# Latent attention pipelined by a group: scores ahead of the older group's values, full-height score products, VectorE normalises

## The chip, the cores and the metric

One of the cores of a Trainium2 chip runs the whole program. The time is the device time of one execution in microseconds (us); lower is better. A core has TensorE (PE; its weight loads are shown apart as PEld), VectorE (DVE), ScalarE (ACT), GpSimd (POOL), SyncE (SP, which here only issues transfers) and 16 DMA engines. TensorE's clock is granted at one of two levels, 1.2 and 2.4 GHz; a mean of 0.5 in a stretch is the lower one throughout.

## The reference, cut to what matters

One layer of a diffusion backbone over 256 context tokens and 1024 latent tokens of width 1024: a windowed grouped-query attention (8 query heads of 64, 2 key groups) and a gated linear recurrence side by side, an output projection, then an expert retrieval that reads, for each token, 128 rows of one table and 128 rows of another. The change touches the attention. For the latent tokens it is

```python
q, k = apply_rope(q), apply_rope(k)
# blocks of 128 queries against the block, its two neighbours (|q - k| <= 128) and 256 cached context keys
s_band = einsum('bnqkgd,bnckd->bkgnqc', qb, k_band) * 64 ** -0.5      # masked outside the window
s_ctx  = einsum('bnqkgd,bckd->bkgnqc', qb, k_ctx) * 64 ** -0.5
p = softmax(concat([s_band, s_ctx, sink]))                            # the sink is a learned logit per head
o = einsum('bkgnqc,bnckd->bnqkgd', p_band, v_band) + einsum('bkgnqc,bckd->bnqkgd', p_ctx, v_ctx)
```

and for the context tokens it is the same over all 256 context tokens, without rotary, window or cache.

## The kernel before

The program is one straight list of instructions, written in this order: the modulation vectors, the context tokens from projection to retrieval (their attention from 125.6 us in the profile), the latent tokens' projection and recurrence (until 518 us), their attention (536.4 to 788.5 us), the output projection `finish` (to about 970 us), the choice of experts, and a long dense stage that computes six of the eight latent tiles' experts with all experts' weights (from about 1790 us to the end). A planner turns the list into one queue for each engine: it takes instructions in the order of the program where their inputs and buffers are ready by its own cost estimates, and so lets later ones go ahead where an engine would idle. On the chip every engine then works its queue in order.

`attend` (lines 385 to 462) does both attentions; `lat` tells them apart. It goes over tiles `t` of 128 queries and over the two key groups `g`. The four heads `c` of a group share its keys. A score product of the latent attention is split for precision: `kh` and `kl` are the high and the low part of the keys (lines 392 to 401), `qs` holds the high part of the queries in the 64 rows of its group and the low part in the other 64 rows (lines 410, 411). A head's scores (128 queries by 640 keys, 512 for the first and the last tile) lie in two PSUM banks. Each bank gets a product of 128 rows, `qs` with `kh`, which holds the keys twice (line 429), and one of 64 rows, high part of `qs` with `kl` (line 430). Two small products add the window's mask (line 433). Then VectorE takes the maximum (436) and makes the bias (437), ScalarE takes the exponential with its sum (438). After four heads the denominator follows (440 to 443), and each head is multiplied by its reciprocal (444 to 448): by `NORM = "AAGV"` the first two on ScalarE, the third on GpSimd, the fourth on VectorE. In the context attention ScalarE does all four.

The second half of a group goes over its blocks of 128 keys (lines 450 to 460): four transposes of probabilities into one PSUM tile `pt`, a copy by ScalarE to `pT`, and a product with the values into `po`. That is called a value step here. The copy of `po` into `qT` (461) ends the group. PSUM is full: three score tiles of two banks, one `pt`, one `po`.

Beside this runs a background stream, `mix` (lines 819 to 851): for four tiles of tokens 256 gather steps each. A step is an indirect transfer of 128 rows of 4 KB, issued by GpSimd (lines 830 and 841), and one VectorE instruction on what has landed (lines 833 and 847). `tick(us)` (lines 110 to 124) decides where in the program these steps stand: it adds to a clock and lets one step go for each 1.9 on it (4.0 in the choice of experts, none while `spread` runs, 2.0 in the dense stage, where the clock starts from 0; lines 53 to 55). The attention ticks 13 after each group (462), `finish` 14 after each tile (525), the choice of experts 13.6 for each of 16 blocks (571). In the dense stage a step's VectorE instruction stands behind the instruction that ticked. What is left in the queue at the end is let go at once (line 1009).

Of the kernel before, what the change touches and what calls it, by code (L numbers as in the profile page):

```python
# [9 lines left out]
F32 = mybir.dt.float32  # L10
# [5 lines left out]
AF = mybir.ActivationFunctionType  # L16
OP = mybir.AluOpType
AX = mybir.AxisListType
# [3 lines left out]
P = 128  # L22
# [14 lines left out]
SCALE = HD ** -0.5  # L37
# [19 lines left out]
E_US = 3.0  # L57
PE_US = 15.8

NORM = "AAGV"  # L60
G_SCALE = 32768.0


# [1 line left out]
def body(ctx: ExitStack, tc: tile.TileContext, i, o):  # L65
    nc = tc.nc
    V, A, T, G = nc.vector, nc.scalar, nc.tensor, nc.gpsimd
# [42 lines left out]
    def tick(us, ins=None):  # L110

        clock[0] += us
        if ins is not None:
            behind.append(ins.ins)
        ph = cur[0]
        step = D_STEP if ph == "dense" else STEP.get(ph, F_STEP)
        while queue and clock[0] >= step:
            try:
                next(queue[0])
                clock[0] -= step  # L120
            except StopIteration:
                queue.pop(0)
        if not queue:
            clock[0] = 0.0
# [213 lines left out]
    def recur(cond, st, ps, gy, xr, blocks=range(4)):  # L338
        lat, _, S, _, _, _, NB = dims(cond)
        for c in blocks:  # L340
# [42 lines left out]
            V.tensor_tensor(hs[0], hs[0], hs[1], op=OP.add)  # L383
            V.tensor_tensor(gy[:, c, :], hs[0], gy[:, c, :], op=OP.mult)
    def attend(cond, st, ps, tiles, qT, kT, vv, spare=None):
        lat, _, S, n, _, _, _ = dims(cond)
        base = S_CTX if lat else 0
        if lat:
            vc = load("vc", [P, 2, P], st)

            flat = [x.rearrange("p k t -> p (k t)") for x in spare]
            kh = flat[0][:, 0:2 * (S + base)].rearrange("p (g k) -> p g k", g=2)
            kl = flat[1][:, 0:S + base]
            qsp = [flat[1][:, S + base + n * 1024:S + base + (n + 1) * 1024].rearrange("p (g c q) -> p g c q", g=2, c=4)
                   for n in range(2)]
            half = [slice(0, 64), slice(64, 128)]
            for src, ks in ((kc, slice(0, base)), (kT, slice(base, base + S))):
                for g in range(2):
                    for r in range(2):
                        A.activation(kh[half[r], g, ks], src[half[g]], AF.Copy)  # L400
                    V.tensor_tensor(kl[half[g], ks], src[half[g]], kh[half[g], g, ks], op=OP.subtract)
        for t in tiles:
            ts = slice(t * P, (t + 1) * P)
            lo, hi = (max(t - 1, 0), min(t + 1, n - 1)) if lat else (0, n - 1)
            W = (hi - lo + 1) * P + base
            nk = W // P
            if lat:
                qs = qsp[t % 2]
                for g in range(2):
                    A.activation(qs[half[g], g], qT[half[g], :, ts], AF.Copy)  # L410
                    V.tensor_tensor(qs[half[1 - g], g], qT[half[g], :, ts], qs[half[g], g], op=OP.subtract)
            for g in range(2):
                gs = slice(g * 64, g * 64 + 64)
                pr = st.tile([P, 4, W], F32, name="pr", bufs=2)
                negm = st.tile([P, 4], F32, name="negm", bufs=2)
                sums = st.tile([P, 4], F32, name="sums", bufs=2)
                den = st.tile([P, 4], F32, name="den", bufs=2)
                for c in range(4):
                    h = g * 4 + c
                    s = ps.tile([P, 2, 512] if lat else [P, W], F32, name="s", bufs=3 if lat else 2)  # L420
                    qh = qT[gs, c, ts]

                    if not lat:
                        T.matmul(s, qh, kT[gs, 0:W], start=True, stop=True)
                    if lat:
                        k0 = base + lo * P
                        for bank, c0, k, w in ((0, 512 - base, 0, base), (1, 0, k0, W - base)):
                            out = s[:, bank, c0:c0 + w]
                            T.matmul(out, qs[:, g, c], kh[:, g, k:k + w], start=True, stop=False, skip_group_check=True)
                            T.matmul(out, qs[gs, g, c], kl[gs, k:k + w], start=False, stop=(bank == 0), skip_group_check=True)  # L430
                        edges = [(blk - lo, mi) for blk, mi in ((t - 1, 0), (t + 1, 1)) if lo <= blk <= hi]
                        for x, (blk, mi) in enumerate(edges):
                            T.matmul(s[:, 1, blk * P:(blk + 1) * P], identb, maskb[:, mi], start=False,
                                     stop=(x == len(edges) - 1), skip_group_check=True)
                        s = s.rearrange("p b w -> p (b w)")[:, 512 - base:512 - base + W]
                    V.reduce_max(den[:, c:c + 1], s, axis=AX.X)
                    V.tensor_scalar(negm[:, c:c + 1], den[:, c:c + 1], -SCALE, nsink[:, h:h + 1], op0=OP.mult, op1=OP.min)
                    A.activation(pr[:, c], s, AF.Exp,
                                 bias=negm[:, c:c + 1], scale=SCALE, accum_out=sums[:, c:c + 1])
                V.tensor_tensor(den, sink[:, g * 4:g * 4 + 4], negm, op=OP.add)  # L440
                A.activation(den, den, AF.Exp)
                V.tensor_tensor(den, den, sums, op=OP.add)
                V.reciprocal(den, den)
                for c in range(4):
                    if not lat or NORM[c] == "A":
                        A.activation(pr[:, c], pr[:, c], AF.Copy, scale=den[:, c:c + 1])
                    else:
                        {"V": V, "G": G}[NORM[c]].tensor_scalar(pr[:, c], pr[:, c], den[:, c:c + 1], None, op0=OP.mult)
                po = ps.tile([P, 4, P], F32, name="po")
                for j in range(nk):  # L450
                    pt = ps.tile([P, 4, P], F32, name="pt")
                    for c in range(4):
                        T.transpose(pt[:, c], pr[:, c, j * P:(j + 1) * P], ident)
                    pT = st.tile([P, 4, P], F32, name="pT", bufs=3)
                    A.activation(pT, pt, AF.Copy)
                    if lat and j < 2:
                        vb = vc[:, j, gs]
                    else:
                        vb = vv[:, lo + j - (2 if lat else 0), gs]
                    T.matmul(po[gs], vb, pT, start=(j == 0), stop=(j == nk - 1))  # L460
                A.activation(qT[gs, :, ts], po[gs], AF.Copy)
                tick(13)

    def finish(es, cond, tiles, qT, gy, dest):

# [224 lines left out]
    ahead = [n * (EARLY // GROUP) % len(order) < EARLY // GROUP for n in range(len(order))]  # L690
# [165 lines left out]
    with ExitStack() as ms:  # L856
# [12 lines left out]
        with ExitStack() as fs:  # L869
# [3 lines left out]
            with ExitStack() as e2:  # L873
                fo = pool(e2, "cfo")
                qT = fo.tile([P, 4, S_CTX], F32, name="qT")
                gy = fo.tile([P, 4, S_CTX], F32, name="gy")
                with ExitStack() as es:
                    fi = pool(es, "cfi")
                    kT = fi.tile([P, S_CTX], F32, name="kT")
                    vv = fi.tile([P, N_CTX, P], F32, name="vv")  # L880
# [16 lines left out]
                    st = pool(es, "cat")  # L897
                    ps = pool(es, "cps", space=PSUM)
# [18 lines left out]
    with ExitStack() as fs:  # L917
        fo = pool(fs, "lfo")
        qT = fo.tile([P, 4, S_LAT], F32, name="qT")
        gy = fo.tile([P, 4, S_LAT], F32, name="gy")  # L920
        with ExitStack() as ks:
            kv = pool(ks, "lkv")
            kT = kv.tile([P, S_LAT], F32, name="kT")
            vv = kv.tile([P, N_LAT, P], F32, name="vv")
# [40 lines left out]
            with ExitStack() as es:  # L965
                attend(1, pool(es, "lat"), pool(es, "lps", space=PSUM), range(N_LAT), qT, kT, vv, (hha, hla))
# [130 lines left out]
```

## Time and profile before

| | us |
|---|---|
| median of 3 runs (lowest, highest) | 3695.29 (3680.69, 3700.97) |
| profiled execution, its own time | 3691.55 |
| span of that execution in the profile | 3689.7 |
| TensorE busy, of the span | 3323.2 (90%) |
| VectorE busy | 3082.3 (84%) |
| GpSimd busy | 1728.7 (47%) |
| ScalarE busy | 1456.6 (39%) |

The span runs from the first to the last instruction. A busy share over the whole program is an average over stages that are limited by different things, so the stages are read one by one. Products on TensorE overlap and their ends are modelled: the distance of two starts tells more than a duration. In a timeline a line is start, duration, engine, line of the kernel, operation, output<-inputs, shape and count, and in brackets how long the engine was idle before it and what ended that.

### The profile page before, as it was taken

The page shows a single profiled execution, that of the slowest core. Times are in us where ns is not written, and L with a number is a line of the kernel's source. Part 1 is how long each engine was busy: PE and PEld are TensorE (multiplying, and loading weights), DVE is VectorE, ACT ScalarE, POOL GpSimd, SP SyncE. Part 2 cuts the span into 40 slices and gives each one's busy share as a digit, 9 for nine tenths or more (in the row PEclk, how much of TensorE's full clock was granted, in tenths as well). Part 3 has the DMA queues.
Part 4 walks back from the last instruction along what each step waited for, and adds up shares of the span by engine and source line. Part 5 has one row for each costly group of instructions (what it writes and reads, how often), then busy time and mean ns, then how long its engine had stood idle before and what let it go on. Part 6 is the DMA issues. An engine that isn't in the chain of part 4 may idle for free.

```text
span 3689.7 us, 48648 instructions
## 1 busy us (share of the span) xinstructions
PE 3323.2 (90%) x16982; PEld 2733.0 (74%) x16982; DVE 3082.3 (84%) x6710; ACT 1456.6 (39%) x2270; POOL 1728.7 (47%) x1162
## 2 busy tenths in 40 slices
PE   7888879888798988889899999989989999999995
PEld 4477654433598877779788888878878888887884
DVE  4549986767799999970699999989989998988898
ACT  5744645533211344542333333433333333333333
POOL 0012454556621121212366666656657666665663
PEclk8799989999899999999999999999999999999998
DMA  8342653568830256773799999988889998988885
GB/s 333 109 158 84 211 201 127 159 233 283 287 97 28 66 152 203 215 218 125 278 346 331 339 341 337 337 307 317 319 300 343 349 344 303 343 303 308 302 317 200
DMA packets 349142, 918.20 MB, mean 249 GB/s; under 512 B 29144, under 2 KB 150104, under 8 KB 345824
## 3 DMA queue, kind: packets, MB, share of 16 engines
q0 software_dynamic: 147456, 536.94, 41.3%
q1 hardware_dynamic: 201440, 378.16, 30.1%
q8 instruction: 133, 2.18, 0.2%
q14 instruction: 113, 0.93, 0.1%
HBM read 834.48 MB, written 80.50 MB: 248 GB/s over the span
## 4 chain that ended last, share of the span: by engine, by line
PE 33%; DVE 24%; issue 6%; DMA 3%; POOL 2%; ACT 1%; POOLq 0%; DVEq 0%; SPq 0%; ACTq 0%
PE u L140 6%; PE u L139 6%; PE u L138 6%; DVE row L833 4%; DVE acc L847 4%; PE rot L138 3%; PE rot L140 3%; PE rot L139 3%; DVE acc L742 2%; DVE oh L676 2%; PE res L138 2%; PE res L140 2%; PE res L139 2%; DVE oh L674 1%; DVE oh L677 1%
## 5 line engine op out<-in xcount | busy, mean ns | idle before, releaser
L830 POOL DMA_INDIRECT row<-in_peer_u,eid x512 | 732.6, 1431 | 571.1 <-DVE row L833 219.0
L841 POOL DMA_INDIRECT row<-in_peer_v,eid x512 | 716.3, 1399 | 493.1 <-DVE acc L847 226.9
L140 PE MATMUL u<-hh,ul 128*128 128x384 f32 x2048 | 709.2, 347 | 59.0 <-DVE ul L135 55.7
L138 PE MATMUL u<-hh,uh 128*128 128x384 f32 x2048 | 709.9, 347 | 6.2 <-ACT a L997 4.4
L139 PE MATMUL u<-hl,uh 128*128 128x384 f32 x2048 | 708.1, 346 | 0.0
L847 DVE SCALAR_TENSOR_TENSOR acc<-row,w,acc 128x1024 f32<-128x1024 f32 x508 | 655.9, 1291 | 25.8 <-DMA row<-in_peer_v,eid 24.3
L833 DVE SCALAR_TENSOR_TENSOR row<-row,h 128x1024 f32<-128x1024 f32 x512 | 623.9, 1233 | 56.6 <-DMA row<-in_peer_u,eid 56.4
L741 ACT ACTIVATE q<-rot 128x512 f32<-128x512 f32 x504 | 298.5, 596 | 479.7 <-PE rot L140 258.6
L140 PEld LDWEIGHTS u<-hh,ul 128*128 128x128 f32 x2048 | 396.7, 194 | 67.7 <-DVE ul L135 59.5
L138 PE MATMUL rot<-vh,ah 128*128 128x512 f32 x1024 | 408.5, 399 | 15.3 <-ACT q L741 14.9
L138 PEld LDWEIGHTS u<-hh,uh 128*128 128x128 f32 x2048 | 397.0, 194 | 14.2 <-ACT a L997 5.7
L139 PE MATMUL rot<-vl,ah 128*128 128x512 f32 x1024 | 400.9, 391 | 0.0
L139 PEld LDWEIGHTS u<-hl,uh 128*128 128x128 f32 x2048 | 396.7, 194 | 5.6
L140 PE MATMUL rot<-vh,al 128*128 128x512 f32 x1024 | 400.8, 392 | 0.0
L742 DVE TENSOR_TENSOR acc<-q,acc 128x512 f32<-128x512 f32 x504 | 342.7, 688 | 13.9 <-ACT q L741 12.4
L135 POOL TENSOR_TENSOR ul<-u,uh 128x1024 fp32r<-128x1024 f32 x44 | 120.6, 2741 | 427.1 <-ACT uh L134 404.2
L138 PE MATMUL mm<-hh,wh 128*128 128x256 f32 (+2 forms) x848 | 288.0, 340 | 12.9 <-ACT wh L134 12.9
L140 PE MATMUL mm<-hh,wl 128*128 128x256 f32 (+2 forms) x848 | 290.3, 343 | 7.4 <-POOL wl L135 4.7
L139 PE MATMUL mm<-hl,wh 128*128 128x256 f32 (+2 forms) x848 | 285.6, 337 | 0.0
L135 DVE TENSOR_TENSOR vl<-v,vh 128x1024 fp32r<-128x1024 f32 x128 | 156.3, 1221 | 120.4 <-DMA gt<-gd 115.9
L134 ACT ACTIVATE uh<-u 128x1024 fp32r<-128x1024 f32 x128 | 135.7, 1061 | 294.2 <-PE u L139 235.5
L138 PEld LDWEIGHTS rot<-vh,ah 128*128 128x128 f32 x1024 | 193.3, 189 | 74.3 <-ACT q L741 36.3
(260 smaller groups left out, 6079.1 us busy)
## 6 DMA issues: line engine op xcount, KB each, us to landing
u<-in_ut SPq DMA_DIRECT2D x128, 512.0 KB
v<-in_peer_v SPq DMA_DIRECT2D x128, 512.0 KB
gd<-stg SPq DMA_DIRECT2D x12, 4096.0 KB
gt<-gd SPq DMA_DIRECT2D x64, 768.0 KB
w<-in_w_mod SPq DMA_DIRECT2D x24, 1024.0 KB
ad<-a SPq DMA_DIRECT2D x88, 192.0 KB
a<-ad SPq DMA_DIRECT2D x44, 384.0 KB
w<-in_w_query SPq DMA_DIRECT2D x32, 512.0 KB
```

Of the source, the lines that this page charges most:

```text
L134: A.activation(hi, src, AF.Copy)
L135: return (eng or V).tensor_tensor(lo, src, hi, op=OP.subtract)
L138: T.matmul(out, lhs[0], rhs[0], start=first, stop=False)
L139: T.matmul(out, lhs[0], rhs[1], start=False, stop=False)
L140: T.matmul(out, lhs[1], rhs[0], start=False, stop=last)
L676: V.tensor_tensor(oh.rearrange(four, j=2), o2.rearrange(four, j=2), pairs(gh, ts), op=OP.mult)
L741: A.activation(q, p, AF.Copy)
L742: tick(share / (2 * (N_DENSE - N_RES)), V.tensor_tensor(y, q, y, op=OP.add))
L830: G.indirect_dma_start(out=u, out_offset=None, in_=i["peer_u"], in_offset=bass.IndirectOffsetOnAxis(ap=eid[:, k:k + 1], axis=0))
L833: V.scalar_tensor_tensor(u, u, 1.0, h2, op0=OP.mult, op1=OP.mult, accum_out=act[:, j:j + 1])
L841: G.indirect_dma_start(out=v, out_offset=None, in_=i["peer_v"], in_offset=bass.IndirectOffsetOnAxis(ap=eid[:, k:k + 1], axis=0))
L847: V.scalar_tensor_tensor(acc, v, w[:, j:j + 1], acc, op0=OP.mult, op1=OP.add)
```

## The change

`attend` is rewritten, in five respects.

1. Its two halves become functions, `scores(t, g)` and `values(t, g, ...)`. The loop calls `scores` for a group and then `values` for the group before it. `pr` (the probabilities of a group) gets three buffers in the latent attention, `pT` two.
2. `kl` becomes as tall as `kh`: the low part of a group's keys is copied to the other 64 rows too, by ScalarE. The second product of a bank takes all 128 rows of `qs`, so it multiplies the low part of the queries with `kl` as well. `qs` of the even tiles moves to the other spare buffer.
3. `NORM` is `"VVVV"`: VectorE normalises all four heads in the latent attention. The context attention keeps ScalarE.
4. One `po` tile serves both groups of a tile of queries, each in its own 64 rows.
5. `tick(13)` after a group becomes `tick(1.6)` after each head and `tick(1.3)` after each value step.

The order of the program changes in the context attention as well.

```diff
-NORM = "AAGV"
+NORM = "VVVV"
...
-            kh = flat[0][:, 0:2 * (S + base)].rearrange("p (g k) -> p g k", g=2)
-            kl = flat[1][:, 0:S + base]
...
+            K2 = 2 * (S + base)
+            kh, kl = (x[:, 0:K2].rearrange("p (g k) -> p g k", g=2) for x in flat)
+            qsp = [x[:, K2:K2 + 1024].rearrange("p (g c q) -> p g c q", g=2, c=4) for x in flat]
...
-                    V.tensor_tensor(kl[half[g], ks], src[half[g]], kh[half[g], g, ks], op=OP.subtract)
+                    V.tensor_tensor(kl[half[g], g, ks], src[half[g]], kh[half[g], g, ks], op=OP.subtract)
+                    A.activation(kl[half[1 - g], g, ks], kl[half[g], g, ks].bitcast(F32), AF.Copy)
...
+        def scores(t, g):
...
+            pr = st.tile([P, 4, W], F32, name="pr", bufs=3 if lat else 2)
...
-                            T.matmul(out, qs[gs, g, c], kl[gs, k:k + w], start=False, stop=(bank == 0), skip_group_check=True)
+                        T.matmul(out, qh, kl[:, g, k:k + w], start=False, stop=(bank == 0), skip_group_check=True)
...
+                tick(1.6)
...
-                        {"V": V, "G": G}[NORM[c]].tensor_scalar(pr[:, c], pr[:, c], den[:, c:c + 1], None, op0=OP.mult)
+                    V.tensor_scalar(pr[:, c], pr[:, c], den[:, c:c + 1], None, op0=OP.mult)
...
+        def values(t, g, pr, lo, nk):
...
+            if g == 0:
+                outs[t] = ps.tile([P, 4, P], F32, name="po")
+            po = outs[t]
...
+                pT = st.tile([P, 4, P], F32, name="pT", bufs=2 if lat else 3)
...
+                tick(1.3)
...
-                tick(13)
...
+        ahead = None
+        for t, g in ((t, g) for t in tiles for g in range(2)):
+            now = scores(t, g)
+            if ahead:
+                values(*ahead)
+            ahead = now
+        values(*ahead)
```

## Rows read from the trace of the kernel before

**Rows 1.** Timeline at the start of the latent attention.
```profile
530.10 4.27 ACT L400 ACTIVATE hh<-kT 64x1024 fp32r<-64x1024 f32 x4
...
536.40 0.58 PE L429 MATMUL s<-hh,hl 128*128 128x256 f32 x1 [16.03 <-DVE hl L411]
```
**Rows 2.** Busy us (instructions) by stage: PE, PEld, DVE, ACT, POOL; clock, DMA share, GB/s.
```profile
125.60:182.70 57.10, 47.49 (x118) 21.50 (x117) 32.76 (x105) 36.63 (x90) 2.20 (x4) 0.61 0.16 51
...
556.70:788.50 231.80, 205.34 (x781) 95.70 (x781) 157.34 (x286) 131.12 (x266) 115.62 (x84) 0.96 0.48 153
...
789.00:1000.00 211.00, 163.42 (x504) 91.98 (x502) 155.21 (x264) 61.16 (x116) 136.34 (x105) 0.90 0.86 293
1000.00:1600.00 600.00, 546.81 (x3986) 502.14 (x3985) 584.67 (x2692) 222.97 (x301) 127.58 (x54) 0.96 0.45 134
3643.00:3690.00 47.00, 14.53 (x54) 10.96 (x54) 38.90 (x59) 15.74 (x28) 15.91 (x9) 0.70 0.23 90
```
**Rows 3.** Timeline, weight loads of one head's scores and of the next one's first.
```profile
646.52 0.19 PEld L429 LDWEIGHTS s<-hh,hl 128*128 128x128 f32 x1
...
647.52 0.18 PEld L430 LDWEIGHTS s<-hl 64*128 64x128 f32 x1 [0.18 <-issue]
...
647.96 0.19 PEld L429 LDWEIGHTS s<-hh,hl 128*128 128x128 f32 x1
```
**Rows 4.** Timeline, weight loads among full-height products: of 256 columns, then of 384.
```profile
1131.07 0.19 PEld L139 LDWEIGHTS mm<-hl,wh 128*128 128x128 f32 x1
...
1131.19 0.19 PEld L140 LDWEIGHTS mm<-hh,wl 128*128 128x128 f32 x1
...
1999.87 0.19 PEld L139 LDWEIGHTS u<-hl,uh 128*128 128x128 f32 x1
...
2000.04 0.19 PEld L140 LDWEIGHTS u<-hh,ul 128*128 128x128 f32 x1
```
**Rows 5.** Timeline, a value step near the end of the latent attention, no scores left.
```profile
782.68 1.07 PE L460 MATMUL po<-pT,vc 128*64 128x512 f32 x2 [0.75 <-ACT pT L455]
...
783.68 0.42 PEld L453 LDWEIGHTS pt<-ident,pr 128*128 128x128 f32 x4 [0.81 <-issue]
...
784.43 0.60 ACT L455 ACTIVATE pT<-pt 128x512 f32<-128x512 f32 x1 [1.81 <-PE pt L453]
...
785.08 1.07 PE L460 MATMUL po<-pT,vv 128*64 128x512 f32 x2 [0.75 <-ACT pT L455]
```
**Rows 6.** By operation, 534 to 790 us: busy, mean ns | idle before, what ended it.
```profile
L448 POOL TENSOR_SCALAR pr<-pr,den 128x640 f32<-128x640 f32 x12 | 28.1, 2341 | 22.2 <-DVE den L443 13.8 <-DVE negm L437 8.2
...
L448 DVE TENSOR_SCALAR pr<-pr,den 128x640 f32<-128x640 f32 x12 | 9.6, 796 | 0.0
```
**Rows 7.** Timeline, one normalise on VectorE that begins before GpSimd's.
```profile
637.48 0.55 DVE L448 TENSOR_SCALAR pr<-pr,den 128x640 f32<-128x640 f32 x1
```
**Rows 8.** Timeline, SyncE issues the loads of the context tokens' output weights.
```profile
182.70 4.11 SPq L476 DMA_DIRECT2D w<-in_w_out  x8
```
**Rows 9.** Timeline, the last gather product on VectorE.
```profile
3646.40 1.28 DVE L847 SCALAR_TENSOR_TENSOR acc<-row,w,acc 128x1024 f32<-128x1024 f32 x1
```
**Rows 10.** Waits, 789 to 935 us: total us, times, longest.
```profile
DVE acc L847 <- DMA row<-in_peer_v,eid: 18.1, 15, 4.1
...
DVE row L833 <- DMA row<-in_peer_u,eid: 16.1, 13, 2.9
```
**Rows 11.** VectorE in the attention: L833 (product and its accumulator read), then L847.
```profile
536.40:788.50 252.10, 38.93 (x64) 0.93 0.47 151
...
536.40:788.50 252.10, 51.47 (x40) 0.93 0.47 151
```
**Rows 12.** Timeline of the context attention, at the lower clock: value products, then transposes.
```profile
151.37 1.97 PE L460 MATMUL po<-pT,vv 128*64 128x512 f32 x2
153.27 1.12 PE L453 MATMUL pt<-ident,pr 128*128 128x128 f32 x4
```
**Rows 13.** Busy us by stage, as in rows 2, of 15 us in the latent attention.
```profile
737.00:752.00 15.00, 15.00 (x42) 6.85 (x43) 6.95 (x17) 5.32 (x12) 5.71 (x4) 0.66 0.44 140
```

More of the change, by code (lines that the diff above doesn't have):

```diff
@@ L387, in attend @@
         base = S_CTX if lat else 0
+        half = [slice(0, 64), slice(64, 128)]
         if lat:
@@ L391, in attend @@
             flat = [x.rearrange("p k t -> p (k t)") for x in spare]
-            kh = flat[0][:, 0:2 * (S + base)].rearrange("p (g k) -> p g k", g=2)
-            kl = flat[1][:, 0:S + base]
-            qsp = [flat[1][:, S + base + n * 1024:S + base + (n + 1) * 1024].rearrange("p (g c q) -> p g c q", g=2, c=4)
-                   for n in range(2)]
-            half = [slice(0, 64), slice(64, 128)]
+            K2 = 2 * (S + base)
+            kh, kl = (x[:, 0:K2].rearrange("p (g k) -> p g k", g=2) for x in flat)
+            qsp = [x[:, K2:K2 + 1024].rearrange("p (g c q) -> p g c q", g=2, c=4) for x in flat]
             for src, ks in ((kc, slice(0, base)), (kT, slice(base, base + S))):
@@ L400, in attend @@
                         A.activation(kh[half[r], g, ks], src[half[g]], AF.Copy)
-                    V.tensor_tensor(kl[half[g], ks], src[half[g]], kh[half[g], g, ks], op=OP.subtract)
-        for t in tiles:
+                    V.tensor_tensor(kl[half[g], g, ks], src[half[g]], kh[half[g], g, ks], op=OP.subtract)
+                    A.activation(kl[half[1 - g], g, ks], kl[half[g], g, ks].bitcast(F32), AF.Copy)
+        def scores(t, g):
             ts = slice(t * P, (t + 1) * P)
@@ L405, in attend @@
             W = (hi - lo + 1) * P + base
-            nk = W // P
-            if lat:
+            gs = half[g]
+            if lat and g == 0:
                 qs = qsp[t % 2]
[L409 to L417, printed above, removed]
-                for c in range(4):
[L419 to L429, printed above, removed]
-                            T.matmul(out, qs[gs, g, c], kl[gs, k:k + w], start=False, stop=(bank == 0), skip_group_check=True)
[L431 to L447, printed above, removed]
-                        {"V": V, "G": G}[NORM[c]].tensor_scalar(pr[:, c], pr[:, c], den[:, c:c + 1], None, op0=OP.mult)
[L449 to L461, printed above, removed]
-                tick(13)
@@ new lines, in scores @@
+                for g2 in range(2):
+                    A.activation(qs[half[g2], g2], qT[half[g2], :, ts], AF.Copy)
+                    V.tensor_tensor(qs[half[1 - g2], g2], qT[half[g2], :, ts], qs[half[g2], g2], op=OP.subtract)
+            pr = st.tile([P, 4, W], F32, name="pr", bufs=3 if lat else 2)
+            negm = st.tile([P, 4], F32, name="negm", bufs=2)
+            sums = st.tile([P, 4], F32, name="sums", bufs=2)
+            den = st.tile([P, 4], F32, name="den", bufs=2)
+            for c in range(4):
+                h = g * 4 + c
+                s = ps.tile([P, 2, 512] if lat else [P, W], F32, name="s", bufs=3 if lat else 2)
+                if not lat:
+                    T.matmul(s, qT[gs, c, ts], kT[gs, 0:W], start=True, stop=True)
+                if lat:
+                    qh = qsp[t % 2][:, g, c]
+                    k0 = base + lo * P
+                    edges = [(blk - lo, mi) for blk, mi in ((t - 1, 0), (t + 1, 1)) if lo <= blk <= hi]
+                    for bank, c0, k, w in ((0, 512 - base, 0, base), (1, 0, k0, W - base)):
+                        out = s[:, bank, c0:c0 + w]
+                        T.matmul(out, qh, kh[:, g, k:k + w], start=True, stop=False, skip_group_check=True)
+                        T.matmul(out, qh, kl[:, g, k:k + w], start=False, stop=(bank == 0), skip_group_check=True)
+                    for x, (blk, mi) in enumerate(edges):
+                        T.matmul(s[:, 1, blk * P:(blk + 1) * P], identb, maskb[:, mi], start=False,
+                                 stop=(x == len(edges) - 1), skip_group_check=True)
+                    s = s.rearrange("p b w -> p (b w)")[:, 512 - base:512 - base + W]
+                V.reduce_max(den[:, c:c + 1], s, axis=AX.X)
+                V.tensor_scalar(negm[:, c:c + 1], den[:, c:c + 1], -SCALE, nsink[:, h:h + 1], op0=OP.mult, op1=OP.min)
+                A.activation(pr[:, c], s, AF.Exp,
+                             bias=negm[:, c:c + 1], scale=SCALE, accum_out=sums[:, c:c + 1])
+                tick(1.6)
@@ new lines, in scores @@
+            V.tensor_tensor(den, sink[:, g * 4:g * 4 + 4], negm, op=OP.add)
+            A.activation(den, den, AF.Exp)
+            V.tensor_tensor(den, den, sums, op=OP.add)
+            V.reciprocal(den, den)
+            for c in range(4):
+                if not lat or NORM[c] == "A":
+                    A.activation(pr[:, c], pr[:, c], AF.Copy, scale=den[:, c:c + 1])
+                else:
+                    V.tensor_scalar(pr[:, c], pr[:, c], den[:, c:c + 1], None, op0=OP.mult)
+            return t, g, pr, lo, W // P
@@ new lines, in attend @@
+        outs = {}
+        def values(t, g, pr, lo, nk):
+            ts = slice(t * P, (t + 1) * P)
+            gs = half[g]
+            if g == 0:
+                outs[t] = ps.tile([P, 4, P], F32, name="po")
+            po = outs[t]
+            for j in range(nk):
+                vb = vc[:, j, gs] if lat and j < 2 else vv[:, lo + j - (2 if lat else 0), gs]
+                pt = ps.tile([P, 4, P], F32, name="pt")
+                for c in range(4):
+                    T.transpose(pt[:, c], pr[:, c, j * P:(j + 1) * P], ident)
+                pT = st.tile([P, 4, P], F32, name="pT", bufs=2 if lat else 3)
+                A.activation(pT, pt, AF.Copy)
+                T.matmul(po[gs], vb, pT, start=(j == 0), stop=(j == nk - 1))
+                tick(1.3)
+            A.activation(qT[gs, :, ts], po[gs], AF.Copy)
```

## The prediction

> **What bounds the kernel now.** I read the page first, then the busy time by stage, then the timeline of the stage that the change rewrites, then the lists by operation and by wait. The latent attention begins with a score product at 536.40 us [rows 1] and ends at 788.5 us. In its main part, 231.8 us, TensorE is busy for 205.3 us, VectorE for 157.3 and ScalarE for 131.1 [rows 2]: TensorE bounds it. The reader should see three things in its timeline.
>
> First, the products of one head take 1.44 us from weight load to weight load, and the half-height load among them starts 0.18 us late with nothing for it to wait for but TensorE's own running product [rows 3]: products of full and of half height do not overlap. Elsewhere, where all are of full height, a 256-column product follows the last after 0.12 us and a 384-column one after 0.17, although each brings a weight load of 0.19 us [rows 4]. Secondly, where no scores are left to fill the gaps, a value step (four transposes, ScalarE's copy, the pair of value products) takes 785.08 - 782.68 = 2.40 us, with the copy of 0.60 us between transposes and product [rows 5]. Thirdly, the stage has 76 such steps (6 query tiles x 2 groups x 5 key blocks, and 2 x 2 x 4 at the edges): a step takes 231.8 / 76 = 3.05 us now. In the timeline the score products already stand between the value steps of the older group, though the program writes them later: the planner overlaps them today as well.
>
> What a step needs of TensorE now: 1.00 us for the products (782.68 to 783.68) and 0.42 for the loads of the transposes [rows 5], plus 64 heads / 76 x 1.44 = 1.21. That is 2.63; it takes 3.05, so 0.42 us stay unfilled.
>
> **The change part by part.** *Full-height products.* A head becomes 2 x 0.12 + 2 x 0.17 = 0.58 us by [rows 4], and its two mask products, which I take at up to 0.22: 0.80 us. A step then needs 1.42 + 0.84 x 0.80 = 2.09 us of TensorE. That is under the 2.40 of the bare chain, which becomes the floor. With the unfilled 0.42 added to the need it would be 2.51. There are no fewer products; low part of q times low part of k is added, at no column.
>
> *The copies for it.* kl gets a second half: four more ScalarE copies ahead of the first product, two of 256 columns and two of 1024. One of 1024 costs 4.27 / 4 = 1.07 us [rows 1]; one of 256 I estimate at 0.43: 3.0 us. TensorE already waits 16.03 us there [rows 1], so they lie on the path. Against that the first four heads are shorter, each by about 1 us at the low clock of that stretch. The 20.3 us from 536.4 to the first transposes at 556.7 change by between -7 and +3; I take -2.
>
> *VectorE normalises all four heads.* ScalarE loses two passes of each group, GpSimd one of up to 2.34 us, for whose input it idles while gathers queue behind it [rows 6]. Neither engine sets the end, so nothing is gained there directly. VectorE gets 48 passes more: 36 of 640 elements at 0.55 us, as one takes when GpSimd isn't at its own pass [rows 7], and 12 of 512 at some 0.48: 25.6 us. Its 12 present passes of 640 average 0.80 us [rows 6] as GpSimd works beside them; without that they save about 3. Net +22 us, 0.29 per step. VectorE's need per step rises from 157.3 / 76 = 2.07 to 2.36. Queued behind four normalises (2.2 us) on VectorE are the next group's maxima, which free the score buffers, and the gather products; three score buffers and a group of lead cover that. But at 2.5 us a step VectorE is 94% busy where it was 68%. I take a step at 2.55: the 2.51 and a little for this. Main part: 76 x 2.55 = 194, so **-38 us**; the ends are 2.40, which gives -49, and 2.86 (below), which gives -14.
>
> *Order and buffers.* Scores of the next group now have the earlier place in the program; the third pr buffer holds what is ahead. The value output is one bank for both groups of a tile, so the next tile's first product waits for ScalarE's copy out of it, as each group's does now. pT with two buffers suffices, since the one pt buffer lets only one step be under way. These I cost at nothing, the score products hide them; without that cover the copy of about 0.6 us would show once per tile, 5 us in all.
>
> *The context attention* (125.6 to 182.7 us) gets the new order too, not the other edits. It runs at a mean clock of 0.61 with TensorE busy for 47.5 of 57.1 us [rows 2], beside the preparation of the latent tokens. Its end matters: the loads of w_out are issued at 182.70 [rows 8]. The idle 9.6 us bound the gain, near enough; I take -4 (-12 to +3).
>
> *Gathers one by one.* The ticks of the stage fall from 16 x 13 = 208 to 64 x 1.6 + 76 x 1.3 = 201.2. At 1.9 a step, with the 112 of the next stage, and then 217.6 at 4.0, 222 gather steps are let go before the dense stage now and 218 then. The four go to the end of the dense stage, whose ticks (1629 at 2.0) have 814 places for 802 steps now, 806 then. VectorE works for 38.9 of the last 47 us [rows 2], and the last gather product stands at 3646.40 [rows 9], just ahead of the closing sums: four more at 1.28 us land among these. **+5 us** (0 to +6). Before that, a shorter attention leaves the background gathers less room. What doesn't fit falls into stages where the DMA engines are 86% busy (789 to 1000 us) or VectorE 97% (1000 to 1600) [rows 2]: +4 (0 to +20).
>
> **Sum**: -38 - 2 - 4 + 5 + 4 = -35 us. The profiled execution took 3691.55 us, 3.7 below the median of 3695.29; so 3656.5 for it and **3660 us** for the median.
>
> **The rivals.** *VectorE binds.* In the stage after the attention VectorE waits 18.1 + 16.1 us for gathers to land [rows 10], over 65 steps: 0.5 us each. The attention has 32 + 40 = 72 steps [rows 11]. If VectorE's crowded queue waited as long there, a value step would take 2.36 + 0.50 = 2.86 us: -14 - 2 - 4 + 5 + 4 = -11, so 3684. For it: 94% busy. Against it: the attention moves 153 GB/s, the stage after it 293 [rows 2], so gathers should land sooner.
>
> *The floor is reached*: 2.40 a step, -7 at the start, -12 in the context attention, no later loss: -63, so 3632.
>
> *It doesn't do what it says.* If a weight load can't run beside a product in the same rows of the array, the heads keep 1.44 us, and the planner overlaps as before: +3 for the copies, -4, +5: 3699. The loads of [rows 4] speak against it. By the Trainium skill, TensorE: Matmul & The Clock Gate, section The mechanism, a load overlaps a running product only where the two use different row groups; [rows 4] show 0.19 us loads of one row group at a spacing of 0.12 us, so this trace does not agree.
>
> *Slower: the clock.* With less work TensorE may fall to the lower level (1.2 GHz). At that level a pair of value products takes 1.97 us and four transposes 1.12 [rows 12], so with the copy a step takes some 3.8, which is 1.25 over my 2.55. The gain is gone once 28 of the 76 steps run so; with half of them the time is 3695 + 12 = 3707. For it: the stage falls today too, to 0.66 from 737 to 752 us [rows 13]. Against it: the last steps, which have no scores, keep the 2.40 us of the higher level (2.4 GHz) [rows 5].
>
> **How the numbers follow.** Forecast 0.64 (its own range 3642 to 3676), VectorE 0.18, floor 0.07, not as said 0.05, clock 0.06. Half a per cent, about what a measurement of this kernel tells from no change, is 18.5 us: faster is below 3677. Faster: 0.64 + 0.07 + 0.03 of VectorE's = 0.74. Same: 0.15 of VectorE's, 0.03 of not as said, 0.01 of the clock = 0.19. Slower: 0.02 + 0.05 = 0.07. The range reaches from 3634, by the floor, to 3694; it leaves out most of not as said, the clock, and half of the floor, some 0.15.
>
> **What would show it.** Right: heads at 0.7 to 0.8 us between weight loads, value steps at 2.4 to 2.6 us, the attention ending near 750 us with VectorE over 85% busy in it, and four more gather products among the last sums. Wrong: score products that still start a load apart, VectorE waiting for gathers as a main row of the attention, a granted clock well under 0.9 after 565 us, or a stage after it that is longer by what the attention gained.

## The result, and the profile after

| | before | after |
|---|---|---|
| median, us (lowest, highest) | 3695.29 (3680.69, 3704.49) | 3719.88 (3715.02, 3728.34) |
| ratio, 95% interval | | 1.0072 (1.0043 to 1.0101) |
| profiled execution, its own time | 3691.55 | 3722.71 |
| latent attention, first score product to the start of the last copy of qT | 252.2 | 224.9 |
| dense stage, start of the first to start of the last accumulation (L742 before, L757 after) | 1848.8 | 1900.0 |
| start of the last accumulation to the end of the span | 26.6 | 35.4 |

The kernel is slower, by 0.7%, where the forecast was 35 us faster, with a chance of 0.74 for faster and 0.07 for slower. The attention did become shorter, by 27 us. All of that, and more, is lost 1000 us later, in a stage of which no line was changed.

Busy time by stage of the kernel after (columns as in [rows 2]): context attention, main part of the latent attention, the stage after it, choice of experts, end.
```profile
125.60:182.70 57.10, 48.88 (x128) 23.46 (x126) 35.26 (x111) 38.17 (x92) 2.20 (x4) 0.60 0.20 62
549.40:761.90 212.50, 177.78 (x784) 86.14 (x783) 161.78 (x325) 109.79 (x236) 72.35 (x59) 0.93 0.48 147
762.00:975.00 213.00, 164.09 (x514) 93.57 (x513) 158.51 (x271) 61.95 (x116) 135.89 (x107) 0.89 0.86 292
975.00:1575.00 600.00, 546.16 (x4017) 500.73 (x4015) 587.86 (x2710) 225.44 (x303) 130.13 (x58) 0.97 0.47 139
3675.00:3721.00 46.00, 8.14 (x35) 6.04 (x33) 36.67 (x59) 13.61 (x24) 17.98 (x9) 0.63 0.27 103
```
The main part of the attention takes 212.5 us in place of 231.8 (232.5 to the end of its last copy, at 789.2), with TensorE busy for 28 us less. The two stages behind it keep their loads. The first accumulation of the dense stage comes at 1785.6 us, where it came at 1814.3: 28.7 us ahead. The last comes at 3685.6, where it came at 3663.1: 22.5 us behind. So the dense stage takes 51 us more, its end 9 more: -28.7 + 51.2 + 8.8 = +31.3, the difference of the two spans (3689.7 and 3721.0).

Timeline of the kernel after, inside the attention: first score product and one of the copies for it, the weight loads of one head's four score products, and the first transposes of two value steps in a row (they answer [rows 1], [rows 3] and [rows 5]).
```profile
536.41 1.06 ACT L402 ACTIVATE hl<-hl 64x1024 fp32r<-64x1024 f32 x1
536.46 0.58 PE L430 MATMUL s<-hh 128*128 128x256 f32 x1 [16.67 <-DVE hh L413]
...
641.05 0.19 PEld L430 LDWEIGHTS s<-hh,hl 128*128 128x128 f32 x1
641.16 0.19 PEld L431 LDWEIGHTS s<-hl 128*128 128x128 f32 x1
641.28 0.19 PEld L430 LDWEIGHTS s<-hh,hl 128*128 128x128 f32 x1
641.40 0.19 PEld L431 LDWEIGHTS s<-hl 128*128 128x128 f32 x1
...
647.72 0.66 PE L464 MATMUL pt<-ident,pr 128*128 128x128 f32 x4
650.12 0.66 PE L464 MATMUL pt<-ident,pr 128*128 128x128 f32 x4
```
The four loads of a head, spread over 1.00 us before (646.52 to 647.52 in [rows 3]), now follow each other after 0.11 to 0.12 us, and no idle time stands among them. A step with a whole head in it takes 650.12 - 647.72 = 2.40 us: the bare chain of [rows 5], the floor. Of the 75 distances from one step's first transposes to the next one's, 50 are 2.5 us or less, where 31 were before.

The same stage from the first transposes, cut in two (columns as above), and the timeline towards its end.
```profile
549.40:710.00 160.60, 140.94 (x678) 71.03 (x677) 125.24 (x256) 93.81 (x201) 43.36 (x39) 1.00 0.41 125
710.00:755.00 45.00, 31.84 (x91) 13.26 (x89) 32.42 (x63) 13.87 (x32) 23.95 (x18) 0.66 0.65 209
...
737.92 1.12 PE L464 MATMUL pt<-ident,pr 128*128 128x128 f32 x4
737.99 0.21 DVE L437 TENSOR_SCALAR negm<-den,nsink 128x1 f32<-128x1 f32 x1
741.68 1.12 PE L464 MATMUL pt<-ident,pr 128*128 128x128 f32 x4
742.89 0.60 ACT L466 ACTIVATE pT<-pt 128x512 f32<-128x512 f32 x1 [2.49 <-PE pt L464]
743.39 0.68 ACT L438 ACTIVATE pr<-s,negm 128x512 f32<-128x512 f32 x1
746.04 0.19 ACT L442 ACTIVATE den<-den 128x4 f32<-128x4 f32 x1
746.27 0.16 DVE L443 TENSOR_TENSOR den<-den,sums 128x4 f32<-128x4 f32 x1 [3.61 <-ACT den L442]
748.70 1.67 DVE L449 TENSOR_SCALAR pr<-pr,den 128x512 f32<-128x512 f32 x4
749.33 1.57 PE L464 MATMUL pt<-ident,pr 128*128 128x128 f32 x4 [3.82 <-DVE pr L449]
```
Most of what is missed of the floor is missed at the end. For 45 us the mean granted clock is 0.66; the transposes of a step take 1.12 us, as in [rows 12] at 1.2 GHz, and a step takes 3.76. The last group's transposes wait 3.82 us for the normalises on VectorE. These had waited for ScalarE's part of den (3.61 us) and then for the two gather products that stand between 746.35 and 748.70. ScalarE in turn took the group's last exponential only at 743.39, behind the copy of an older value step, though VectorE had made its bias by 738.2.

And the dense stage: busy time (columns as above; the window is from the first to the last accumulation) in the kernel before and in the one after.
```profile
1814.00:3663.00 1849.00, 1755.59 (x8393) 1538.69 (x8391) 1704.46 (x2192) 676.75 (x1030) 1147.51 (x793) 0.98 0.89 322
```
```profile
1786.00:3686.00 1900.00, 1770.55 (x8390) 1547.06 (x8388) 1701.74 (x2192) 672.12 (x1026) 1154.88 (x793) 0.97 0.88 314
```
VectorE has the same work, 1702 to 1704 us; the 51 us are idle time on it (144.5 us before, 198.3 after). TensorE, which is fuller still, stands idle for 93.4 us before and 129.5 after. The question for the runs was what makes that idle time.

### The profile page after: what moved, and what is told of

It reads as the page before. It is cut to its first block, busy times and chain, and to the rows that moved or that the text cites. A ratio compares the mean times of both kernels' runs of the same rounds, so it can differ in the third digit from the quotient of the medians.

```text
span 3721.0 us, 48584 instructions
## 1 busy us (share of the span) xinstructions
PE 3299.7 (89%) x16982; PEld 2729.4 (73%) x16982; DVE 3087.8 (83%) x6758; ACT 1434.6 (39%) x2242; POOL 1696.7 (46%) x1146
## 4 chain that ended last, share of the span: by engine, by line
DVE 27%; PE 26%; issue 8%; DMA 4%; POOL 4%; ACT 1%; SPq 0%; POOLq 0%; DVEq 0%; ACTq 0%
DVE acc L862 5%; PE u L140 5%; DVE row L848 5%; PE u L139 5%; PE u L138 5%; DVE acc L757 3%; PE rot L138 2%; PE rot L140 2%; PE rot L139 2%; DMA row<-in_peer_u,eid 2%; DVE oh L691 2%; POOL row L856 2%; DVE oh L692 1%; DVE oh L689 1%; PE res L140 1%
## 5 line engine op out<-in xcount | busy, mean ns | idle before, releaser
L757 DVE TENSOR_TENSOR acc<-q,acc 128x512 f32<-128x512 f32 x504 | 341.8, 686 | 13.1 <-ACT q L756 12.5
```

The costliest lines, as they stand in the source:

```text
L757: tick(share / (2 * (N_DENSE - N_RES)), V.tensor_tensor(y, q, y, op=OP.add))
```

## The experiments

**Where the dense stage loses.** The two kernels with the number of gather steps exchanged. After with 222:
```diff
             ahead = now
         values(*ahead)
+        if lat:
+            tick(6.8)
```


> The kernel after, with 6.8 more ticks at the end of its latent attention, so that 222 gather steps are let go ahead of the dense stage as before, where the kernel after lets 218 go; nothing else. Theory A (the attention gained some 28 us, and the dense stage loses some 50 and the end some 9 because the gather stream stands four steps further back against the groups of the dense stage): the dense stage takes 1849 us again, first accumulation to last, and the time is some 3660 us, ratio 0.990 to 0.993. Theory B (the dense stage is slower for another reason that comes with the attention's code: other instructions ahead of it in the queues, other buffers, the gathers' later times): the dense stage keeps its 1900 us and the time stays at 3715 to 3722, ratio 1.006.

Before with 218:
```diff
-                tick(13)
+                tick(12.575)
```


> The kernel before, with the tick of each attention group at 12.575 in place of 13, so that 218 gather steps are let go ahead of the dense stage; the attention's instructions are those of before. Theory A: the dense stage takes some 1900 us in place of 1849 and the end 35 in place of 27, so some 3750 us, ratio 1.014 to 1.017. Theory B: 3690 to 3701, ratio 1.000.

Measured: after with 222 steps 3661.56 us, ratio 0.9907 (0.9871 to 0.9942); before with 218 steps 3748.91 us, 1.0145 (1.0107 to 1.0183). The dense stage takes 1847.5 and 1895.3 us. Theory A holds both ways: the loss belongs to the four steps and not to the attention. VectorE's order of instructions in the dense stage, read from the traces, is the same to 99.8% for equal numbers of steps, whatever the attention; with 218 against 222 less than half of it agrees.

**Count or place.** Is fewer steps the better, or is it a matter of where they fall? (A batch is 16 gather steps on one table; 16 on the other make the pair. A block is one of the 128 blocks of experts that the dense stage goes through, two by two, and two of them are a group. The high part of a block's first weights is uh, made by ScalarE; VectorE makes the low part, ul, from it. The rotating sums, rot, take turns in two PSUM buffers, and ScalarE copies them out.) Four steps more and eight fewer than 222 (`tick(14.4)` in place of `tick(6.8)`; `tick(1.2)` in place of `tick(1.3)`):

> The kernel after, with 14.4 more ticks at the end of its latent attention: 226 gather steps ahead of the dense stage, four more than before. Theory A1 (what costs is where the stream's batch ends and tile ends fall among the instructions of a group): the time has no slope in the number of steps, anything from 3650 to 3725 us, and other groups of the dense stage are the long ones than with 218 and with 222. Theory A2 (every step taken out of the dense stage saves a share, the fewer the better): some 13 us for each step as between 218 and 222, so some 3610 us. Theory A3 (a threshold, such as the last batch falling behind the last accumulations): the time of 222, 3655 to 3665.

> The kernel after, with 1.2 in place of 1.3 for the tick of a value step: 214 gather steps ahead of the dense stage, four fewer than the kernel after. Theory A1: no slope, anything from 3655 to 3725. Theory A2: some 55 us more than after, 3770. Theory A3: the time of after or a little more, 3715 to 3735.

Then single steps (`tick(4.8)`, `tick(8.5)`, `tick(11)`) and a whole batch pair of 32 (`tick(67.8)`):

> The kernel after with 4.8 more ticks at the end of its attention: 221 gather steps ahead of the dense stage. Theory S1 (a region of the phase is good): the dense stage within 15 us of the 1848 of 222. Theory S2 (one lucky step): 1885 to 1920 us, as with 218.

> The same with 8.5 more ticks: 223 steps. Theory S1: within 15 us of 1848. Theory S2: 1885 to 1925 us, as with 226.

> The same with 11 more ticks: 224 steps, the dense stage begins at the end of a batch. Theory S1: 1848 to 1885 us, half-way to 226 at most. Theory S2: 1885 to 1925 us.

> The same with 67.8 more ticks: 254 steps, so that batches of 16 end where they end with 222, and a tile ends 32 steps earlier; the dense stage has 32 steps fewer, some 40 us of VectorE, which are missing in its last groups. Theory B1 (the place of the batch ends decides): from its 8th to its 100th block the dense stage takes what it takes with 222, to within 15 us, and the whole dense stage some 1805 to 1850 us. Theory B2 (the places of the tile ends decide, or every place counts): 20 to 60 us more up to the 100th block, the whole at 1860 to 1900 us.

| steps ahead of the dense stage | dense stage, us | VectorE waits for uh, us | time, us |
|---|---|---|---|
| 214 | 1903.4 | 136.6 | 3728.73, ratio 1.0073 (1.0045 to 1.0101) |
| 218 (after) | 1900.0 | 129.1 | 3719.88 |
| 221 | 1835.3 | 74.4 | 3645.66, one execution |
| 222 | 1847.5 | 82.3 | 3661.56 |
| 223 | 1894.9 | 133.4 | 3718.52, one execution |
| 224 | 1865.9 | 80.0 | 3670.76, one execution |
| 226 | 1921.0 | 160.1 | 3746.47, ratio 1.0137 (1.0092 to 1.0182) |
| 254 | 1881.2 | 133.4 | 3718.69, one execution |

Beside the four kernels with one execution the kernel before took 3692.70 us. There is no slope. A2 falls with both runs. A3 falls with 226 (it wanted 3655 to 3665), though 214 lies in its range. A1's "no slope" is what is left, but both times lie above its upper end, 3725. One step is worth up to 47 us, and 221 and 222 are the best of the eight; the kernel before stands on one of them. With 254, where batches end in the same places as with 222, the stretch from the 8th to the 100th block takes 1401 us against 1357: B1 falls too, and both ranges of B2 hold. S1 holds for 221 and for 224 (1848 to 1885), S2 for 223, so neither holds for all three. Of no rule of place can I say that it was shown: why one order leaves more idle time than another stays open.

**What the idle time is.** Waits in the dense stage (total us, times, longest) of the kernel after with 222 steps, then of after itself.
```profile
DVE ul L135 <- ACT uh L134: 82.3, 21, 9.4
PE u L140 <- DVE ul L135: 55.7, 9, 9.0
```
```profile
DVE ul L135 <- ACT uh L134: 129.1, 28, 9.5
PE u L140 <- DVE ul L135: 82.7, 14, 8.7
PE rot L138 <- ACT q L756: 30.6, 24, 6.0
```
A piece of after's dense stage, by engine:
```profile
2118.95 1.28 DVE L862 SCALAR_TENSOR_TENSOR acc<-row,w,acc 128x1024 f32<-128x1024 f32 x1
2120.14 1.22 DVE L135 TENSOR_TENSOR ul<-u,uh 128x1024 fp32r<-128x1024 f32 x1
2121.41 0.69 PE L140 MATMUL u<-hh,ul 128*128 128x384 f32 x1 [5.88 <-DVE ul L135]
...
2131.79 1.06 ACT L134 ACTIVATE uh<-u 128x1024 fp32r<-128x1024 f32 x1 [3.22 <-PE u L139]
2132.88 1.23 DVE L135 TENSOR_TENSOR ul<-u,uh 128x1024 fp32r<-128x1024 f32 x1 [5.67 <-ACT uh L134]
```
Twice in 12 us an engine waits for another that was itself held up. TensorE waits 5.88 us for ul, whose input uh had been there since before 2100 us; VectorE stood at accumulations and gather products. Then VectorE waits 5.67 us for uh, as its two buffers are free only when TensorE has read one.

So I gave uh and ul a third buffer, to see whether those buffers are the cause:
```diff
-N_MORE = 3
+N_MORE = 2
...
+        turns[0] += 1
+        if third and turns[0] % 3 == 2:
+            uh = third[0].tile([P, KD, P], F32R, name="uh", bufs=1)
+            ul = third[0].tile([P, KD, P], F32R, name="ul", bufs=1)
+        else:
+            uh = eu.tile([P, KD, P], F32R, name="uh", bufs=2)
+            ul = eu.tile([P, KD, P], F32R, name="ul", bufs=2)
...
+            third.append(pool(es, "eu3"))
```


> The kernel after (218 steps) with a third buffer for the two parts of an expert's first weights (uh, ul) in the dense stage; the room comes from two row buffers of the second pool in place of three and from moving the masks. Theory U (the dense stage loses where two blocks' parts stand ready and the third must wait until TensorE has read the first, with VectorE and then TensorE waiting behind: VectorE's wait for uh is 129 us with 218 steps against 82 with 222): the dense stage falls from 1900 to 1845 to 1865 us, that wait to under 60 us. Rival (the loss lies in other waits, those for the copies of the rotating sums or for the gathers): 1890 to 1905 us, the wait for uh may shrink but another takes its place.

The control has N_MORE = 2 and the moved masks alone:

> The control of the run with the third buffer: the kernel after with two row buffers in the second pool in place of three and the masks moved, and still two buffers for uh and ul. Expected: the dense stage at 1895 to 1925 us (a row buffer fewer can only hold the gathers back), the time 3715 to 3745. If it falls to 1865 or less by itself, the place of every gather product among the groups decides, and the run with three buffers shows nothing about them.

Waits in the dense stage of the control, then with the third buffer.
```profile
DVE ul L135 <- ACT uh L134: 127.7, 27, 9.2
DVE row L848 <- DMA row<-in_peer_u,eid: 40.0, 25, 5.1
PE u L140 <- DVE ul L135: 87.4, 14, 9.7
PE rot L138 <- ACT q L756: 37.1, 28, 7.2
PE res L138 <- ACT ah L134: 10.8, 7, 3.0
```
```profile
DVE row L857 <- DMA row<-in_peer_u,eid: 94.2, 49, 5.8
DVE ul L135 <- ACT uh L134: 87.0, 25, 8.4
PE rot L138 <- ACT q L765: 58.8, 27, 8.1
PE res L138 <- ACT ah L134: 43.5, 20, 6.5
PE u L140 <- DVE ul L135: 34.6, 5, 10.8
```
Theory U falls, and the rival's range (1890 to 1905) is missed too. TensorE's wait for ul shrinks by 52.8 us, its waits for the copies of the rotating sums and for ah grow by 21.7 + 32.7 = 54.4, and VectorE waits 54 us more for gathers. The dense stage takes 1925.0 us against 1911.8 of the control; the times are 3749.91 (1.0142, 1.0117 to 1.0167) and 3739.39 (1.0103, 1.0080 to 1.0127). The wait for uh goes roughly with the length in the table above (224 steps have less of it than 222 and a longer stage), but it is not shown to be its cause: the third buffer changes VectorE's order again, and the idle time moves to other waits. What the buffer would do in an unchanged order was not measured.

**What each part does to the attention.** The first three of these kernels have 222 steps, so that their dense stage stays as it was. Full height alone, in the kernel before:
```diff
-            kl = flat[1][:, 0:S + base]
+            kh, kl = (x[:, 0:K2].rearrange("p (g k) -> p g k", g=2) for x in flat)
...
+                    A.activation(kl[half[1 - g], g, ks], kl[half[g], g, ks].bitcast(F32), AF.Copy)
...
-T.matmul(out, qs[gs, g, c], kl[gs, k:k + w], ...)
+T.matmul(out, qs[:, g, c], kl[:, g, k:k + w], ...)
```


> The kernel before, with the full-height score products alone (kl in both halves, four more ScalarE copies); order, ticks (222 steps) and the normalising as before. If TensorE's half-height products were the bound of the attention: most of the 28 us that the attention of the kernel after is shorter, so some 3668 to 3675 us, ratio 0.992 to 0.995. If the order of scores and products is what gives the gain: 3690 to 3698, no change, with heads that run faster and wait longer for the buffers.

VectorE's normalising alone (`NORM = "VVVV"` in the kernel before):

> The kernel before, with VectorE normalising all four heads and nothing else (222 steps). If TensorE's products bound the attention: no change, 3690 to 3700 us. If the slow normalise on GpSimd, 2.34 us, held up the transposes: 5 to 12 us less, 3683 to 3690. If VectorE is near its limit in the attention: 5 to 20 us more.

Everything but that (`NORM = "AAGV"` in the kernel after, 222 steps):

> The kernel after with the normalising split over the engines as before (two heads on ScalarE, one on GpSimd, one on VectorE) and 6.8 more ticks at the end of the attention (222 steps): what is left of the change is the full-height products, the new order and the gathers one by one. If the four normalises on VectorE cost the same in this order as in the order of before (attention 252 to 265 us there), the attention takes some 211 us and the time is 3645 to 3652. If the new order hides the normalises, so that full height and order are what they are in the kernel after: attention 222 to 226 us, 3658 to 3665.

And the kernel after with `tick(0)` in its attention:

> The kernel after with ticks of 0 in the latent attention: none of the 104 gather steps is let go there, all come later, so that only the attention itself is to be read (224.9 us in the kernel after, from its first score product to the last copy of qT). Theory Q (VectorE's queue holds the attention up: the maxima and normalises stand behind each other and behind the gather products, 76 us of them): the attention falls to 200 to 212 us. Theory L (the way from score to transposes is longer now, whatever else VectorE does): 218 to 225 us. The whole time is of no account here: more gathers than the dense stage has places for.

Busy time in the whole attention, first score product to the end of the last copy: before, full height alone, VectorE's normalising alone, after, after without VectorE's normalising, after with `tick(0)`; each from its own trace, columns as above.
```profile
536.40:789.20 252.80, 225.23 (x826) 106.88 (x827) 171.19 (x315) 142.14 (x289) 120.74 (x87) 0.93 0.47 151
```
```profile
541.90:752.90 211.00, 178.35 (x826) 92.31 (x827) 169.06 (x315) 142.75 (x290) 121.29 (x87) 0.96 0.55 178
```
```profile
532.10:797.70 265.60, 229.47 (x825) 107.65 (x826) 182.12 (x358) 119.65 (x257) 78.99 (x66) 0.90 0.43 137
```
```profile
536.40:761.90 225.50, 187.50 (x826) 94.76 (x827) 173.80 (x351) 119.84 (x256) 75.16 (x61) 0.91 0.48 149
```
```profile
535.40:744.90 209.50, 176.69 (x826) 91.32 (x827) 164.28 (x311) 142.00 (x290) 117.55 (x83) 0.96 0.55 174
```
```profile
525.20:730.40 205.20, 177.02 (x826) 91.72 (x827) 156.00 (x320) 119.49 (x256) 53.85 (x46) 0.96 0.39 123
```
The parts add up to within 3 us. Full height alone takes 42 us off (TensorE is busy for 47 less), more than either of its two answers, and the kernel is at 3650.91 us, ratio 0.9878 (0.9840 to 0.9915). By the medians that is more than the whole change gains with 222 steps; the intervals of the two ratios overlap. VectorE's normalising alone adds 13 us, the third of its answers: 3711.73, ratio 1.0039 (1.0011 to 1.0068). In the new order it adds 225.5 - 209.5 = 16, the first answer of the two that were written down: the order doesn't hide it. The new order with the gathers one by one is worth 211.0 - 209.5 = 1.5 us here. That is not told from nothing: nine kernels with the attention of after take 223.7 to 228.7 us for it.

With `tick(0)` 47 gather products stand in the attention in place of 63, and with all four normalises on VectorE it takes 204.6 us from product to the start of the last copy (one execution): theory Q's range. So the way through four normalises is not dear by itself; it is together with the gather work in the same queue. (`tick(0)` takes the gathers' transfers and GpSimd's part away as well, so that it is VectorE's queue alone is argued, not shown.)

**Put together**: the kernel after without VectorE's normalising has 3650.66 us with 222 steps, ratio 0.9855 (0.9825 to 0.9885). With the 221 of the table (`tick(4.8)`):

> The kernel after with the normalising split as before (two heads on ScalarE, one on GpSimd, one on VectorE) and 4.8 more ticks at the end of the attention, so 221 gather steps ahead of the dense stage. If the two are independent: the dense stage takes 1832 to 1840 us, the attention 207 to 212, and the time is 3635 to 3645, ratio 0.983 to 0.987. If the good place of 221 hangs on the attention's own code: dense 1848 or more, 3650 or more.

Measured: dense stage 1840.6 us, attention 209.0, time 3643.82, ratio 0.9843 (0.9806 to 0.9880): both findings hold side by side. It has the lowest ratio of the kernels that were timed over several rounds, but its interval overlaps that of 222 steps, so the gain of 221 over 222 shows in the dense stage and not in the time.

## Why the prediction was wrong

**The step that failed** is "Gathers one by one", the +5 us (0 to +6). I counted the four steps rightly, 222 and 218, and asked only what they cost where they end up. There it was somewhat low: from the last accumulation to the end it takes 8.8 us more, over the upper end of 6, and these rows of after stand where [rows 9] stood.
```profile
3680.34 1.28 DVE L862 SCALAR_TENSOR_TENSOR acc<-row,w,acc 128x1024 f32<-128x1024 f32 x1
...
3685.01 1.29 DVE L757 TENSOR_TENSOR acc<-q,acc 128x512 f32<-128x512 f32 x2
```
What I left out is that with four steps fewer ahead of it every one of the other 800 meets a different group of the dense stage, and that the planner then writes another order for a stage of 1849 us, in which VectorE was busy for 92% and TensorE for 95%. That stage became 51 us longer. Against 222 steps, a shift of one to eight moves it by -12 to +74 us. No term and none of my rivals had this; of my signs of being wrong, only the longer stage after the attention comes near it, and I gave it no price. The profile told how full the engines are there. My bound of 0 to +6 was a bound on the work moved, not on the stage it was moved past.

**The main term** (-38, ends -49 to -14) came to 212.5 - 232.5 = -20.0, both from the first transposes to the end of the last copy: 2.80 us a step in place of 2.55. Its mechanism was right: the loads overlap, a step reaches the floor, and full height alone gives 197.2 us for the 76 steps, 2.59 each. Mis-sized was VectorE's normalising. The passes cost what I took for them:
```profile
L449 DVE TENSOR_SCALAR pr<-pr,den 128x640 f32<-128x640 f32 x48 | 24.2, 566 | 0.0
L449 DVE TENSOR_SCALAR pr<-pr,den 128x512 f32<-128x512 f32 x16 | 6.7, 480 | 0.0
```
But I let 0.04 us a step stand for their place in the queue, and it is some 0.2 on the mean. It does not fall on every step. The first 60 steps take 154.2 us in the kernel after and 156.5 without VectorE's normalising; the 15 distances behind them take 55.2 and 36.1. In the old order VectorE's normalising alone turns 188.8 into 190.2 and 40.6 into 51.6. So "three score buffers and a group of lead cover that" was right for most of the stage and failed at its end, where the last groups lose their lead. In the kernel without VectorE's normalising the last group's den is complete 12.8 us ahead of its first transposes, in the kernel after 3.1 us ahead (746.27 and 749.33 above):
```profile
721.76 0.16 DVE L443 TENSOR_TENSOR den<-den,sums 128x4 f32<-128x4 f32 x1
...
734.55 0.66 PE L464 MATMUL pt<-ident,pr 128*128 128x128 f32 x4
```
What takes that lead is not shown to the last link: the wait ran through ScalarE's queue as well as through VectorE's. I looked at VectorE's share, which I put at 94% and which is 161.78 / 212.5 = 76%. A share of 76% leaves room on the mean, not in the order. Taking three of four normalises off VectorE gives the time back, and so does taking 16 gather products out. It is the two together, and not that gathers crowd at the end: in the 40 us ahead of the last normalise stand 15 of them in the kernel after and 17 in the one without VectorE's normalising, which loses nothing there. The rival "VectorE binds" (2.86 a step) was nearer to this than the forecast, though it looked for waits on transfers, which are 5.9 us in all here.

**Right or near**: the start (20.3 us become 12.9; -7.4, just past the end of -7 to +3); the copies, 1.06 us for 1024 columns; the context attention, -6.8 in these two traces (I took -4), and 42 to 50 us in all kernels with its new order against 52 to 57 in those without, though the latent attention began at 536.4 us in both of these two; order and buffers at nothing (-1.5). Give-back, +4 (0 to +20), is about nothing: from the start of the attention's last copy to the first accumulation 1025.7 us before and 1024.3 after, with gathers waited for a little less than in [rows 10]:
```profile
DVE row L848 <- DMA row<-in_peer_u,eid: 14.7, 13, 3.0
DVE acc L862 <- DMA row<-in_peer_v,eid: 13.3, 16, 3.0
```
**The rivals.** "Not as said" is out: the loads of one row group stand 0.11 us apart. By the Trainium skill, TensorE: Matmul & The Clock Gate, section The mechanism, a load overlaps a running product only where the two use different row groups; this trace does not agree. The clock did fall, for the 45 us from 710 to 755. Steps took 3.76 us there, where I had worked out 3.8, but that stretch holds 11 steps and not 28. That the kernel after with 222 steps has 3661.56 us, next to the 3660 of the forecast, is partly chance: without the +5 my sum gives 3655, with a gain too large in the attention and differences ahead of it: over all kernels the latent attention begins between 521.5 and 541.9 us.

## What to carry to other kernels

When a change lets background work go in another rhythm, even by four steps of a thousand, the order of everything behind it is written anew; price that stage by a range taken from its idle time on the fullest engine, or keep the number and place of the background steps when comparing. Judge each part with the rest held still: here one part gave 42 us, another took 13 to 16, and a side effect of the pacing took 60. For an engine that shares its queue with background work, price what is added by the order in the queue, and at the end of the stage, where no later group stands ahead to cover a wait; a share of 76% said nothing of its cost.

## What the runs showed of the hardware that was not expected

With the same order of instructions the dense stage takes the same time to within 6 us (1846.5 to 1852.2 in five kernels with 222 steps, 1895.3 and 1900.0 with 218), although the executions as wholes differ by more. And where TensorE had to wait at the end of the attention, the mean granted clock went to 0.66 (31.84 us of work in 45). The clock is not what sets the time there, as far as two traces tell: the kernel after with 222 steps has the same attention, 224.2 us, with 0.85 over the like 45 us (695 to 740) and longer waits in its place (TensorE busy for 25.93).
